# The order of TensorE and VectorE written out for the last depthwise tile and the layer norm behind it

## The chip, the cores and the metric

The kernel runs on one core of a Trainium2 chip, as one program. The metric is the device time of one execution, in microseconds (us), as the median of the runs shown. TensorE is called PE, VectorE DVE, ScalarE ACT, GpSimd POOL and the engine that issues the DMAs SP, as the profile calls them.

## The reference, cut to what matters

One step of a hybrid backbone of two layers with model width 1024, over 1024 sample tokens and 128 prompt tokens. Layer 0 mixes with a Conformer convolution, layer 1 with attention; both have a convolutional feed-forward behind the mixer. The change is in the Conformer mixer of layer 0:

```
def layernorm(x, g, b):
    mu = mean(x, -1)
    xc = x - mu
    y = xc * rsqrt(mean(xc * xc, -1) + EPS)
    return y * g + b

def conformer_conv(h, w_pw1, dw_w, dw_b, ln_g, ln_b, w_pw2):
    a, g = split(h @ w_pw1, 2, axis=-1)        # 1024 -> 2 x 1024
    u = a * sigmoid(g)
    u = dwconv(u, dw_w, dw_b)                  # 31 taps over the tokens, per feature
    u = silu(layernorm(u, ln_g, ln_b))         # mean and variance over the 1024 features
    return u @ w_pw2                           # 1024 -> 1024
```

Around it: `h = modulate(rmsnorm(x, norm1_g), sh1, sc1)`, then `x = x + g1 * y`. The vectors `sh1, sc1, g1, ...` of both layers come from `silu(cond) @ ada_w + ada_b` (adaLN).

## The kernel before, in words

**Layout.** Features lie on the partitions, tokens along the columns. The 1152 tokens are cut into three chunks of 384 (`c` = 0, 1, 2), the 1024 features into eight tiles of 128 (`j` = 0 to 7). Chunk 2 holds the last 256 sample tokens and the 128 prompt tokens. Products of weights take three matrix products each, high and low parts in a rounded float32 format (`mm3`, L247 to L249): one product of a tile with one chunk has 3 x 8 = 24 entries on PE. The products of the depthwise taps, of the means and of adaLN are in plain float32; each stands in the trace as two entries.

**The stage.** For each feature tile `gated(j, c)` computes the two pointwise products and the gated tile `u`. Then the 31 taps of the tile are summed: for tiles 0 to 6 the first 19 on DVE into `da` (L658, L660, all tokens at once, 1167 columns with the padding between samples and prompt), the other 12 on ACT and POOL into `pacc` (L645 to L651), and `join` (L666) adds the two into `U[c][:, j]`. `da` lies in a PSUM slot of which there is one (`acc`), so a tile's taps begin when the tile before is joined.

Tile 7, the last, is cut differently. 16 of its taps are products with diagonal matrices on PE (`diag`, L699; `dl`, L706), one PSUM bank per chunk; DVE adds seven taps on top of them (L660, `dl`), 384 columns a chunk (399 for chunk 2), ACT and POOL do eight (`pacc7`).

**The norm of a chunk.** The mean over the features is eight products with a matrix of 1/1024 (`mu`): those of tiles 0 to 6 in a loop ahead of the norm (L722, called the mean's head here, 14 entries), that of tile 7 in `layer_norm` (L726, the mean's tail, 2 entries). Then DVE subtracts the mean in two halves of four tiles (L731), ACT squares (L738), DVE and POOL add the squares (L741, L744), PE sums them over the partitions (`token_rstd`, L325, 12 entries), DVE scales (L332), POOL takes the power -1/2 (L334), PE spreads the result to all partitions (`spread`, L342, 6 entries), DVE multiplies (L753), ACT does Silu with gain and bias (L757) and a copy that is the high part `ln_h` (L760), and DVE subtracts it for the low part `ln_l` (L762). With both parts the last products of the mixer start (`pw2p`, eight feature tiles `m` for each chunk), with the residual on DVE (L384).

PSUM has in this stage four banks under `mm` (`dl` of three chunks, the mean of chunk 0, the sums of each norm, and then the `pw2p` products), one slot of three banks under `acc` (`da`, later the means of chunks 1 and 2) and one bank under `ms` (adaLN).

**What sets the order.** A planner at build time places the instructions on each engine by its own model of the times and by their order in the program; on the chip each engine then takes them in that fixed order and waits by semaphores. `tc.manual_schedule(engines=...)` keeps the program's order for the instructions that stand inside it on the engines named. In the kernel before it is used for SP in the whole program and for PE in the attention. The norms are generators in a list `bg`; `tick()` lets each take one step, and it is called after each of tile 7's taps on DVE and after each product:

```
    for c in range(NCH):
        for _ in taps_vector(last, u, dl[c], te, *SPAN[c], False):
            tick()
        join(last, dl[c], pacc, c, SPAN[c][0])
        bg.append(layer_norm(c))
        if c == 0:
            tick()
```

The adaLN products (`ada`, L270) of later layers run in the same stage, as their weights arrive (L258), and were traced ahead of it; so were the splits of weights into high and low parts (L220 on ACT, L221 on DVE) up to the first of `pw2p`; the later ones are traced behind it.

Of the kernel before, what the change touches and what calls it, by code (L numbers as in the profile page):

```python
# [11 lines left out]
ALU = mybir.AluOpType  # L12
# [55 lines left out]
def pieces(c):  # L68
    """A chunk's columns by the conditioning of their tokens."""
    lo, hi = c * CH, (c + 1) * CH  # L70
    out = []
    if lo < NS:
        out.append((0, min(hi, NS) - lo, 0))
    if hi > NS:
        out.append((max(lo, NS) - lo, CH, 1))
    return out
# [3 lines left out]
def tile_hybrid_step(ctx: ExitStack, tc: tile.TileContext, a: dict, outs: list):  # L80
# [17 lines left out]
    def phase(**slots):  # L98
        """SBUF of a phase: so many tiles of so many columns for each tag."""
        stack = ExitStack()  # L100
        pools = {
            tag: (stack.enter_context(tc.tile_pool(name=f"s_{tag}", bufs=bufs, reuse_waits="tile")), n)
            for tag, (bufs, n) in slots.items()
        }

        def tile_(tag, name, dt=F32, n=None):
            pool_, cols_ = pools[tag]
            return pool_.tile([P, n or cols_], dt, tag=tag, name=name)

        return stack, tile_  # L110
# [15 lines left out]
    class Banks:  # L126
        """PSUM, cut anew for some phases."""

# [16 lines left out]

    # work that runs beside the products, a step after each of them
    bg = []
# [22 lines left out]

    # ---- weights, in the order of their use: loads run up to three tiles ahead, the split into hi + lo (both exact
    # in float32r) one or two ----
    def ffn_order(l):
# [25 lines left out]
    class Weights:  # L199
# [24 lines left out]
        def ahead(self, splits, loads):  # L224
            """Has everything up to so many tiles from the next one split or loaded."""
            for i in range(self.at, min(self.at + max(splits, loads), len(self.order))):
                if self.order[i][0] == "stop":
                    break
                if i < self.at + loads and i not in self.raw and i not in self.ready:
                    self.load(i)  # L230
                if i < self.at + splits and i not in self.ready:
                    self.split(i)
# [17 lines left out]

# [1 line left out]
    def ada(pool, l, grp):  # L252
# [55 lines left out]

# [1 line left out]
    def add_stat(acc, j, c, src, eng=None, tag=None):  # L310
# [8 lines left out]
    def token_rstd(pool, parts, name, bank=None):  # L319
        """Sums over features of all parts[f, token], then (mean + eps) ** -0.5, tokens on partitions."""  # L320
        n = CH // P
        ps = pool("ms", f"{name}_s") if bank is None else bank[:, CH:]
        for t in range(n):
            for i, x in enumerate(parts):
                nc.tensor.matmul(  # L325
                    ps[:, t : t + 1], x[:, t * P : (t + 1) * P], ones, start=(i == 0), stop=(i == len(parts) - 1)
                )
        return rstd_of(ps[:, 0:n], 1.0 / D, n, name)
# [8 lines left out]
    def spread(pool, v, name, bank=None):  # L337
        """v[token, t] to every partition, tokens along the columns."""
        n = v.shape[1]
        ps = pool("ms", f"{name}_b") if bank is None else bank  # L340
        for t in range(n):
            nc.tensor.matmul(  # L342
                ps[:, t * P : (t + 1) * P], v[:, t : t + 1].to_broadcast([P, P]), ident, start=True, stop=True
            )
        return ps[:, 0 : n * P]
# [44 lines left out]

# [1 line left out]
    def ffn(pool, H, X, l, name, beside, done):  # L392
# [87 lines left out]

    # =========================== layer 0 ===========================
    pool.open(mm=(4, 512), acc=(1, 1536), ms=(1, 512))

# [1 line left out]
    vec_rows = [  # L485
# [36 lines left out]
    def load_x(c):  # L522
        """A chunk's tokens, on partitions, where the low parts of the normed chunks go later."""
        n = CH // P
        toks = hp.tile([P, n, D], F32, tag="hl", name=f"xt{c}")
        for t in range(n):
            tt = c * n + t
            nc.sync.dma_start(
                toks[:, t, :], a["x_sample"][0, tt * P : (tt + 1) * P, :] if tt < NS // P else a["x_prompt"][0]
            )  # L530
        return toks
# [45 lines left out]

    # conformer: gated pointwise, depthwise over tokens, layernorm, silu, pointwise
    us = []

    def gated(j, c):
        """The products of a chunk; yields before their gating."""
        if c == 0:
# [58 lines left out]
    def taps_pool(j, u, pacc, t0, s0_, s1_):  # L642
        """The taps from t0 on, with the bias."""
        d = pacc[:, s0_:s1_]
# [8 lines left out]
    def taps_vector(j, u, d, n, s0_, s1_, fresh):  # L653
        """The first n taps."""
        for t in range(n):
# [15 lines left out]
    for j in range(last + 1):  # L671
# [14 lines left out]
        taps_pool(j, u, pacc, t0, 0, CONV_N)  # L686
        for _ in taps_vector(j, u, da[:, 0:CONV_N], t0, 0, CONV_N, True):
            pass
        for c in range(NCH):
            join(j, da, pacc, c)  # L690

    # the last tile: some taps as products with diagonals, the others on top of them, chunk by chunk, so that the norm
    # of a chunk runs beside the taps of the next
    u = us[last][2]
# [5 lines left out]
    dl = []  # L700
    for c in range(NCH):
        s0_, s1_ = SPAN[c]
        dl.append(pool("mm", f"dl{c}")[:, 0 : s1_ - s0_])
        for i in range(PE_TAPS):
# [3 lines left out]
            )  # L708

    L = [None] * NCH  # L710
    half = KT // 2
    mus = []
    for c in range(NCH):
        if c == 0:
# [6 lines left out]
        for j in range(last):  # L721
            nc.tensor.matmul(mus[c], mean_w, U[c][:, j, :], start=(j == 0), stop=False)  # L722

    def layer_norm(c):
# [4 lines left out]
        for g in range(2):  # L729
# [3 lines left out]
            )  # L733
            eng = (nc.vector, nc.gpsimd)[g]
            for i in range(half // 2):
                sq = slot("tmp", f"lnsq{c}_{g}_{i}")[:, 0 : 2 * CH]
# [8 lines left out]
            yield  # L745
        yield
        bank = pool("mm", f"lnv{c}")
        rs = token_rstd(pool, ss, f"lnv{c}", bank)
        yield
        pb = spread(pool, rs, f"lnv{c}", bank)  # L750
        for g in range(2):
            jj = slice(g * half, (g + 1) * half)
            nc.vector.tensor_tensor(  # L753
                U[c][:, jj, :], U[c][:, jj, :], pb.unsqueeze(1).to_broadcast([P, half, CH]), ALU.mult
            )
            for j in range(g * half, (g + 1) * half):
                nc.scalar.activation(  # L757
                    U[c][:, j, :], U[c][:, j, :], AF.Silu, scale=col("conv_ln_g", j), bias=col("conv_ln_b", j)
                )
            nc.scalar.activation(hh[:, jj, :], U[c][:, jj, :], AF.Copy)  # L760
            yield
            nc.vector.tensor_tensor(hl[:, jj, :], U[c][:, jj, :], raw32(hh)[:, jj, :], ALU.subtract)  # L762
# [5 lines left out]
    for c in range(NCH):  # L768
# [4 lines left out]
        if c == 0:  # L773
            tick()

    def project_residual(H, X, c, acc, l, name, tag):
# [29 lines left out]

    # =========================== layer 1 ===========================
    # rotary tables with the norm gains folded in, tokens on partitions; gains: plain, halves swapped and signed
    NB = NS // P + 1
# [59 lines left out]
    def head_norm(ps, which, tt, name):  # L869
        """RMS norm of two heads, rotary unless they are the prompt's; yields between its stages."""  # L870
        ss = tiny(f"{name}ss", 2)
# [37 lines left out]
    def place(b, tt, o):  # L909
        """Heads to [feature, token]."""  # L910
        pt = pool("t", f"ptqk{b}_{tt}")
# [14 lines left out]

    # each slot: the products of a tile, then a further stage of each tile before it, the oldest first
    stages = []
# [50 lines left out]

    # the prompt's queries see the prompt's own keys: the four heads of a group at once  # L980
    def prompt():
# [54 lines left out]

    # samples: blocks of one head and the queries of one chunk, in steps of 128 queries; the scores run two steps
    # ahead of the transposes, the product with V one block behind them
    blocks = [(c, h) for c in range(NCH) for h in range(NH)]
# [27 lines left out]
    def softmax(s, st):  # L1067
        """Yields before each part of its exponential."""
        v = st["v"]
# [121 lines left out]

    # final norm, back to tokens on partitions
    gfs = []
# [44 lines left out]
def _rope_table():  # L1238
    """cos and sin by position on the 64-wide grid: [128, 2, 9, 32]; block t < 8 is the row part of token tile t,
    block 8 the column part, which all tiles share."""  # L1240
    import numpy as np
# [34 lines left out]
```

## Time and profile before

| | us |
|---|---|
| median of 3 runs | 2791.1 (2790.43 to 2793.83) |
| span of the profiled execution (its own time) | 2789.3 |
| PE busy | 2724.6 (98%) |
| DVE busy | 1585.4 (57%) |
| ACT busy | 1053.5 (38%) |
| POOL busy | 699.6 (25%) |
| the chain that ended last, share on PE | 94% |

The profiled execution has its time shown as a span, from the first to the last instruction; what lies around it is not in the profile. The span is 1.8 us below the median of the runs. Busy shares are means over the whole span, in which stages with different limits follow one another: the stage of the change lies between 333 and 425 us. "Granted clock" is TensorE's clock by the profile, as a share of full speed; its two levels are 1.2 and 2.4 GHz. In a timeline several instructions of one kind in a row are merged (x20 is twenty), and in brackets stands how long the engine had been idle before and what ended that. A few per cent of the matrix products are missing from a trace.

### The profile page before, as it was taken

Reading aid. Unit: us, or ns where it says so; the run is one execution under the profiler, and the core shown is the slowest. Engines: PE = TensorE matmul, PEld = TensorE weight load, DVE = VectorE, ACT = ScalarE, POOL = GpSimd, SP = SyncE. Lnnn points to the kernel's source line nnn. Section 1 sums busy time; section 2 is a strip of 40 time slices with the busy share of each in tenths; the row PEclk is TensorE's granted clock in tenths of the full one; section 3 lists DMA queues with packets and bytes.
Section 4 is the critical chain, followed back from the end, with each engine's and each line's share of the span. In section 5 each row is a group of like instructions: output and inputs, shape, how many; then the busy total and the mean of one; then the engine's idle time right before and its main releaser. Section 6 shows DMA issues by size and latency. Waiting matters only on the chain.

```text
span 2789.3 us, 40007 instructions
## 1 busy us (share of the span) xinstructions
PE 2724.6 (98%) x15959; PEld 2577.1 (92%) x15959; DVE 1585.4 (57%) x2743; ACT 1053.5 (38%) x2066; POOL 699.6 (25%) x782
## 2 busy tenths in 40 slices
PE   7999989999999999999999899999999999999999
PEld 4867649999999999999999799899999999999998
DVE  6878886544444444445643788766544444444445
ACT  5545546422222221222555777755422122221222
POOL 2777744300000000000555566535000000000003
PEclk9999989999999999999999999999999999999999
DMA  7465425311111111111210000044111111111111
GB/s 261 158 185 160 154 91 176 110 32 46 46 46 46 39 46 38 46 38 46 95 58 1 1 1 1 32 129 136 45 40 46 38 46 39 46 39 45 32 53 69
DMA packets 194419, 192.18 MB, mean 69 GB/s; under 512 B 7072, under 2 KB 173323, under 8 KB 192698
## 3 DMA queue, kind: packets, MB, share of 16 engines
q1 hardware_dynamic: 193946, 189.53, 21.7%
q8 instruction: 126, 2.06, 0.3%
q14 instruction: 59, 0.48, 0.1%
q0 software_dynamic: 288, 0.11, 0.0%
HBM read 175.19 MB, written 14.42 MB: 68 GB/s over the span
## 4 chain that ended last, share of the span: by engine, by line
PE 94%; DVE 3%; DMA 1%; ACT 1%; issue 0%; POOL 0%; SPq 0%; DVEq 0%; ACTq 0%; POOLq 0%
PE f1pd L249 3%; PE f1pd L247 3%; PE f1pd L248 3%; PE f1pg L249 3%; PE f0pg L249 3%; PE f1pg L248 3%; PE f0pg L248 3%; PE f0pv L247 3%; PE f0pg L247 3%; PE f1pv L249 3%; PE f1pg L247 3%; PE f0pv L248 3%; PE f1pv L248 3%; PE f1pv L247 3%; PE f0pv L249 3%; PE f0pd L248 3%
## 5 line engine op out<-in xcount | busy, mean ns | idle before, releaser
L220 ACT ACTIVATE w_hi<-w_raw 128x1024 fp32r<-128x1024 f32 x208 | 218.1, 1058 | 939.4 <-PE f0pd L248 223.7
L221 DVE TENSOR_TENSOR w_lo<-w_raw,w_hi 128x1024 fp32r<-128x1024 f32 x208 | 269.4, 1304 | 425.0 <-ACT w_hi L220 422.4
L651 POOL TENSOR_TENSOR pacc<-pacc,tmp 128x1167 f32<-128x1167 f32 (+2 forms) x98 | 234.2, 2393 | 64.8 <-ACT tmp L650 41.6
L384 DVE SCALAR_TENSOR_TENSOR x<-f1pd,mods,x 128x256 f32<-128x256 f32 (+1 forms) x352 | 170.2, 514 | 102.6 <-PE f1pd L249 102.4
L384 DVE SCALAR_TENSOR_TENSOR x<-f0pd,mods,x 128x256 f32<-128x256 f32 (+1 forms) x352 | 169.8, 514 | 99.1 <-PE f0pd L249 98.9
L660 DVE SCALAR_TENSOR_TENSOR da<-u,dww,da 128x1167 f32<-128x1167 f32 x126 | 180.8, 1435 | 2.8
L1084 POOL TENSOR_TENSOR pr<-pr,sm 128x384 f32<-128x384 f32 x192 | 153.8, 829 | 107.3 <-DVE sm L1082 49.4
L411 POOL MEMSET f1gp<- 128x1 f32 x66 | 3.7, 98 | 703.7 <-DVE f1gp L435 690.5
L411 POOL MEMSET f0gp<- 128x1 f32 x66 | 3.6, 98 | 703.8 <-DVE f0gp L435 690.7
L248 PE MATMUL f1pd<-f1al,w_hi 128*128 128x384 f32 x528 | 178.8, 339 | 0.0
L249 PE MATMUL f1pd<-f1ah,w_lo 128*128 128x384 f32 x528 | 178.7, 338 | 0.0
L249 PE MATMUL f0pd<-f0ah,w_lo 128*128 128x384 f32 x528 | 178.7, 338 | 0.0
L248 PE MATMUL f0pd<-f0al,w_hi 128*128 128x384 f32 x528 | 178.5, 338 | 0.0
L247 PE MATMUL f1pd<-f1ah,w_hi 128*128 128x384 f32 x528 | 178.5, 339 | 0.0
L247 PE MATMUL f0pd<-f0ah,w_hi 128*128 128x384 f32 x528 | 178.0, 338 | 0.0
L249 PE MATMUL f0pg<-n_h,w_lo 128*128 128x384 f32 x528 | 176.7, 335 | 0.0
L249 PE MATMUL f1pg<-n_h,w_lo 128*128 128x384 f32 x528 | 176.7, 335 | 0.0
L248 PE MATMUL f1pg<-n_l,w_hi 128*128 128x384 f32 x528 | 176.7, 335 | 0.0
L248 PE MATMUL f0pv<-n_l,w_hi 128*128 128x384 f32 x528 | 176.7, 335 | 0.0
L248 PE MATMUL f0pg<-n_l,w_hi 128*128 128x384 f32 x528 | 176.7, 335 | 0.0
L247 PE MATMUL f0pg<-n_h,w_hi 128*128 128x384 f32 x528 | 176.7, 335 | 0.0
L247 PE MATMUL f1pg<-n_h,w_hi 128*128 128x384 f32 x528 | 176.7, 335 | 0.0
(327 smaller groups left out, 7802.7 us busy)
## 6 DMA issues: line engine op xcount, KB each, us to landing
adaw<-in_ada_w_dram SPq DMA_DIRECT2D x96, 512.0 KB, 4.4
w_raw<-in_ffn_w_up_dram SPq DMA_DIRECT2D x88, 512.0 KB, 3.8
w_raw<-in_ffn_w_down_dram SPq DMA_DIRECT2D x44, 512.0 KB, 3.9
w_raw<-in_conv_w_pw_dram SPq DMA_DIRECT2D x40, 512.0 KB, 6.8
w_raw<-in_attn_w_o_dram SPq DMA_DIRECT2D x24, 512.0 KB, 4.4
xs_d<-x SPq DMA_DIRECT2D x6, 1536.0 KB, 11.1
x<-xs_d SPq DMA_DIRECT2D x6, 1536.0 KB, 7.8
w_raw<-in_attn_w_qkv_dram SPq DMA_DIRECT2D x12, 512.0 KB, 3.6
```

The costliest lines, as they stand in the source:

```text
L220: nc.scalar.activation(hi, raw, AF.Copy)
L221: nc.vector.tensor_tensor(lo, raw, raw32(hi), ALU.subtract)
L247: nc.tensor.matmul(ps, wh, mh, start=first, stop=False)
L248: nc.tensor.matmul(ps, wh, ml, start=False, stop=False)
L249: nc.tensor.matmul(ps, wl, mh, start=False, stop=last)
L384: nc.vector.scalar_tensor_tensor(xx, ps[:, lo:hi], mod(l, v, j, cond), xx, ALU.mult, ALU.add)
L411: nc.gpsimd.memset(gp[:, z : z + 1], 0.0)
L651: nc.gpsimd.tensor_tensor(d, d, tmp, ALU.add)
L660: nc.vector.scalar_tensor_tensor(d, src, tap(j, t), d, ALU.mult, ALU.add)
L1084: nc.gpsimd.tensor_tensor(pr[n], pr[n], ri.to_broadcast([P, CH]), ALU.mult)
```

## The change

The taps of tile 6 on DVE and their joins become a function `on_vector`, which is called inside a new block with the order of DVE and PE written out, `vector`. In that block the program's order is: tile 6's taps and joins; the diagonal products of tile 7 for chunks 0 and 1; the mean's head of chunk 0; tile 7's taps of chunk 0, their join, and the first step of chunk 0's norm (the mean's tail and the subtraction); the diagonal products of chunk 2; the mean's heads of chunks 1 and 2; and then tile 7's taps of chunks 1 and 2 with a step of a norm after each. Before, all diagonal products stood ahead of all mean's heads, and the planner chose the order.

In `layer_norm` the squares alternate between the two halves, with one step for each pair of squares; for chunk 0 the multiplication, the Silu, the copy and the low part go in quarters of two feature tiles instead of halves of four. For chunks 1 and 2 the halves stay. The rest of the diff takes comments and docstrings out.

```diff
--- before
+++ after
@@ -684,13 +684,18 @@
         pacc = slot("pacc", f"pacc{j}")
         t0 = TAPS - (POOL_TAPS if j < last - 1 else POOL_TAPS_6)
         taps_pool(j, u, pacc, t0, 0, CONV_N)
-        for _ in taps_vector(j, u, da[:, 0:CONV_N], t0, 0, CONV_N, True):
-            pass
-        for c in range(NCH):
-            join(j, da, pacc, c)
-
+        def on_vector(j=j, u=u, da=da, pacc=pacc, t0=t0):
+            for _ in taps_vector(j, u, da[:, 0:CONV_N], t0, 0, CONV_N, True):
+                pass
+            for c in range(NCH):
+                join(j, da, pacc, c)
+        if j < last - 1:
+            on_vector()
     u = us[last][2]
     t0 = TAPS - POOL_TAPS_7
     te = t0 - PE_TAPS
@@ -698,7 +703,8 @@
     for i in range(PE_TAPS):
         nc.scalar.activation(diag[:, i, :], ident, AF.Copy, scale=tap(last, te + i))
     dl = []
-    for c in range(NCH):
+    def taps_tensor(c):
         s0_, s1_ = SPAN[c]
         dl.append(pool("mm", f"dl{c}")[:, 0 : s1_ - s0_])
         for i in range(PE_TAPS):
@@ -707,10 +713,19 @@
                 dl[c], diag[:, i, :], u[:, s0_ + t : s1_ + t], start=(i == 0), stop=(i == PE_TAPS - 1)
             )
 
+    vector = ExitStack()
+    vector.enter_context(tc.manual_schedule(engines={mybir.EngineType.DVE, mybir.EngineType.PE}))
+    on_vector()
+    for c in range(NCH - 1):
+        taps_tensor(c)
     L = [None] * NCH
     half = KT // 2
     mus = []
-    for c in range(NCH):
+    def mean_head(c):
+        nonlocal mu_all
         if c == 0:
             mu = pool("mm", "mu0")
         else:
@@ -721,6 +736,9 @@
         for j in range(last):
             nc.tensor.matmul(mus[c], mean_w, U[c][:, j, :], start=(j == 0), stop=False)
 
+    mu_all = None
+    mean_head(0)
     def layer_norm(c):
         mu = mus[c]
         nc.tensor.matmul(mu, mean_w, U[c][:, KT - 1, :], start=False, stop=True)
@@ -731,8 +749,10 @@
             nc.vector.tensor_tensor(
                 U[c][:, jj, :], U[c][:, jj, :], mu.unsqueeze(1).to_broadcast([P, half, CH]), ALU.subtract
             )
-            eng = (nc.vector, nc.gpsimd)[g]
-            for i in range(half // 2):
+        yield
+        for i in range(half // 2):
+            for g in range(2):
+                eng = (nc.vector, nc.gpsimd)[g]
                 sq = slot("tmp", f"lnsq{c}_{g}_{i}")[:, 0 : 2 * CH]
                 j0 = g * half + 2 * i
                 nc.scalar.activation(sq.rearrange("p (j t) -> p j t", t=CH), U[c][:, j0 : j0 + 2, :], AF.Square)
@@ -743,22 +763,30 @@
                     for o in (0, CH):
                         eng.tensor_tensor(ss[g], ss[g], sq[:, o : o + CH], ALU.add)
             yield
-        yield
         bank = pool("mm", f"lnv{c}")
         rs = token_rstd(pool, ss, f"lnv{c}", bank)
         yield
         pb = spread(pool, rs, f"lnv{c}", bank)
-        for g in range(2):
-            jj = slice(g * half, (g + 1) * half)
+        n = 2 if c == 0 else half
+        for j0 in range(0, KT, n):
+            jj = slice(j0, j0 + n)
             nc.vector.tensor_tensor(
-                U[c][:, jj, :], U[c][:, jj, :], pb.unsqueeze(1).to_broadcast([P, half, CH]), ALU.mult
-            )
-            for j in range(g * half, (g + 1) * half):
+                U[c][:, jj, :], U[c][:, jj, :], pb.unsqueeze(1).to_broadcast([P, n, CH]), ALU.mult
+            )
+            for j in range(j0, j0 + n):
                 nc.scalar.activation(
                     U[c][:, j, :], U[c][:, j, :], AF.Silu, scale=col("conv_ln_g", j), bias=col("conv_ln_b", j)
                 )
             nc.scalar.activation(hh[:, jj, :], U[c][:, jj, :], AF.Copy)
-            yield
+            if c or j0 % half:
+                yield
+            if c == 0 and j0:
+                pp = slice(j0 - n, j0)
+                nc.vector.tensor_tensor(hl[:, pp, :], U[c][:, pp, :], raw32(hh)[:, pp, :], ALU.subtract)
+            if c:
+                nc.vector.tensor_tensor(hl[:, jj, :], U[c][:, jj, :], raw32(hh)[:, jj, :], ALU.subtract)
+        if c == 0:
             nc.vector.tensor_tensor(hl[:, jj, :], U[c][:, jj, :], raw32(hh)[:, jj, :], ALU.subtract)
         L[c] = (hh, hl)
 
@@ -772,6 +800,11 @@
         bg.append(layer_norm(c))
         if c == 0:
             tick()
+            taps_tensor(NCH - 1)
+            for i in range(1, NCH):
+                mean_head(i)
+    vector.close()
 
     def project_residual(H, X, c, acc, l, name, tag):
         for m in range(KT):
```

## Rows read from the trace of the kernel before

**Rows 1.** The page's first line.
```profile
span 2789.3 us, 40007 instructions
```
**Rows 2.** Table by stretches: window, busy us and instructions by engine, granted clock, DMA.
```profile
393.00:405.00 12.00, 6.98 (x35) 4.61 (x33) 8.63 (x13) 3.52 (x6) 5.62 (x6) 0.87 0.00 0
405.00:417.00 12.00, 5.86 (x21) 4.89 (x21) 10.06 (x10) 11.95 (x16) 2.05 (x2) 0.50 0.01 2
417.00:429.00 12.00, 11.98 (x55) 11.98 (x56) 6.84 (x6) 8.10 (x11) 0.00 (x0) 0.77 0.84 254
```
**Rows 3.** Timeline of PE: start, us, line, operation, out<-in, count, idle before.
```profile
333.42 3.39 PE L706 MATMUL dl<-u,diag 128*128 128x384 f32 x10
...
340.20 6.72 PE L706 MATMUL dl<-u,diag 128*128 128x384 f32 x20
...
369.64 1.05 PE L270 MATMUL ada<-adaw,cs 128*32 128x512 f32 x4
...
385.32 5.32 PE L722 MATMUL mu<-u,mean_w 128*128 128x384 f32 x16
390.57 1.05 PE L270 MATMUL ada<-adaw,cs 128*32 128x512 f32 x4
...
396.61 1.40 PE L325 MATMUL lnv<-ones,lnss 128*128 128x1 f32 x12
...
405.87 2.29 PE L325 MATMUL lnv<-ones,lnss 128*128 128x1 f32 x10 [0.28 <-POOL lnss L744]
410.19 1.65 PE L342 MATMUL lnv<-ident,lnv_r 128*128 128x128 f32 x6 [2.02 <-POOL lnv_r L334]
414.32 1.33 PE L247 MATMUL pw2p<-ln_h,w_hi 128*128 128x384 f32 x3 [2.48 <-ACT ln_h L760]
417.02 0.69 PE L248 MATMUL pw2p<-ln_l,w_hi 128*128 128x384 f32 x1 [1.37 <-DVE ln_l L762]
...
423.42 0.33 PE L249 MATMUL pw2p<-ln_h,w_lo 128*128 128x384 f32 x1
```
**Rows 4.** Chain that ended last, in order of time: chunk 2's sums and spread.
```profile
437.33 1.01 PE lnv L325 x10
...
442.96 0.67 PE lnv L342 x6
```
**Rows 5.** Timeline of DVE, 336 to 417 us.
```profile
336.26 1.44 DVE L658 TENSOR_SCALAR da<-u,dww 128x1167 f32<-128x1167 f32 x1
337.73 8.81 DVE L660 SCALAR_TENSOR_TENSOR da<-u,dww,da 128x1167 f32<-128x1167 f32 x6
346.44 0.61 DVE L660 SCALAR_TENSOR_TENSOR dl<-u,dww,dl 128x384 f32<-128x384 f32 x1
...
366.35 1.23 DVE L221 TENSOR_TENSOR w_lo<-w_raw,w_hi 128x1024 fp32r<-128x1024 f32 x1
...
378.53 1.54 DVE L666 TENSOR_TENSOR u<-da,pacc 128x384 f32<-128x384 f32 x4
...
404.87 3.42 DVE L753 TENSOR_TENSOR u<-u,lnv 128x1536 f32<-128x1536 f32 x2
...
415.21 3.42 DVE L762 TENSOR_TENSOR ln_l<-u,ln_h 128x1536 fp32r<-128x1536 f32 x2
```
**Rows 6.** Timeline of PE at the end of the attention.
```profile
1834.85 0.42 PE L247 MATMUL wop<-ao_h,w_hi 128*128 128x384 f32 x1
...
1839.18 0.28 PE L247 MATMUL po<-pT_h,vh 128*128 128x256 f32 x1
```
**Rows 7.** Timeline of POOL: the power of chunk 1.
```profile
408.90 1.24 POOL L334 TENSOR_TENSOR lnv_r<-lnv_m,mhalf 128x3 f32<-128x3 f32 x1 [3.08 <-DVE lnv_m L332]
```
**Rows 8.** Timeline of ACT: the Silu and copies of chunk 0.
```profile
406.71 1.28 ACT L757 ACT_TABLE_LOAD   x1
408.00 4.89 ACT L757 ACTIVATE u<-u,vecs 128x384 f32<-128x384 f32 x8
412.80 2.84 ACT L760 ACTIVATE ln_h<-u 128x1536 fp32r<-128x1536 f32 x2
```

## The prediction

> **What bounds the kernel now.** I read the page first: PE is busy almost to the end of a 2789.3 us span [rows 1], so only a stage in which PE stands still can give anything. The table by stretches shows one such stage, the end of the first mixer. Between 393 and 417 us PE is busy 6.98 + 5.86 of 24 us, and the granted clock falls from 0.87 to 0.50, its lower level, and is back at 0.77 over the next stretch [rows 2]. After that PE does not stop before the feed-forward, so whatever is saved here moves the end one for one, unless a new stop appears behind it.
>
> Then PE in order of time [rows 3]. Its last pointwise product ends at 333.42. From there it runs without a gap through the depthwise products of the last tile (`dl`), the adaLN products (`ada`) and the mean products (`mu`) until 396.61, when the sums of chunk 0's norm (`lnv`) begin. From there it waits, by the releasers in brackets, for VectorE, GpSimd and ScalarE in turn; the first `pw2p` product starts at 414.32, goes on at 417.02, and the 24 entries of one product are through at about 423.3.
>
> Of these 26.7 us (396.61 to 423.3) the work itself is, at full clock: sums and spread of chunks 0 and 1, 2 x (1.01 + 0.67) [rows 4]; one mean tail of two entries, 0.65 [rows 3]; 24 product entries at 0.175, 4.2. That is 8.2, so 18.5 us are lost. That is the most that the change can give.
>
> **The change, part by part.**
>
> *Tile 6 first on VectorE.* Now VectorE alternates tile 6's taps (`da`) with tile 7's (`dl`), and tile 6 is joined only at 378.53 [rows 5]. Its taps start at 336.26, behind the join of tile 5, which the change does not touch. With the order written out they run alone: 19 taps at (8.81 - 1.43) / 5 = 1.476, 28.0, to 364.3; four joins, 1.54, to 365.8; seven taps of chunk 0 at about 0.6, 4.2; one join, 0.55: 370.6. Two weight splits (the one shown and another) came ready at 366 to 369. They stand outside the written order. I read what becomes of such instructions from the attention, whose TensorE order is written out too: `wop` products that follow that block in the code run at 1834.85, ahead of `po` products of the block at 1839.18 [rows 6]. So others still slip in between, and I add the two splits, 2.4 together: chunk 0's last mean product can start at about 373.2. Bounds: 370.8 without the splits, 374 with waits beside them.
>
> *PE until then.* Two chunks of `dl`, 64 entries at about 0.333, 21.3; chunk 0's mean head, 14 at 0.325, 4.6; `ada`, whose groups take about 0.98 each and of which nine of 14, the one at 369.64 the ninth, had run by 370, 8.9 [rows 3]; gaps 0.7. From 333.42 this gives 369: PE waits some 4 us that it does not wait today. Bounds: 0, if `ada` fills it, to 5.
>
> *PE behind it, in the written order.* Mean tail 0.65, third chunk of `dl` 32 x 0.345 (399 columns instead of 384) = 11.0, two mean heads 28 x 0.325 = 9.1, five groups of `ada` and its transposes 5.3: 26.1, about 400 for the start of chunk 0's sums. This is the cover that the change puts over the subtraction, squares and sums of chunk 0: from 373.9 these need 3.4 for the subtraction, which has the shape of the multiplication [rows 5], and, as an estimate, four squares and the additions between them some 7, done by about 385.
>
> *Sums to spread.* The sums end at 401.2. For chunk 1 today the sums end at 408.16, the power starts at 408.90 and takes 1.24, and the spread of 1.65 ends at 411.84 [rows 3, 7]: 3.7. With PE at full clock at its start I take 3.5: 404.7. Bounds 2.8 to 3.7.
>
> *Norm in quarters.* Today halves: multiplication 1.7, the eight Silu, both copies, then the low part 1.7 [rows 5, 8]. The change has quarters of 768 columns: multiplication 0.87, two Silu 1.25, copy 0.78, so the first high part is there 3.0 after the spread, the first low part 3.9 after. The later quarters follow at ScalarE's pace, two Silu and a copy, 1.95; the last low part is at 9.75. PE is fed six entries per quarter; at the low clock it needs 1.92 for them, so it is just kept busy. I let the low clock last until the fourth quarter; the last six then take about 1.2: 24 entries done 11.1 after the spread, 415.8. Bounds: 10.7 if the clock never falls, and 2.5 us more than I take if 17 further entries run at 0.32 instead of 0.175, as they do from 417.02 today.
>
> The table load of 1.28 ahead of the first Silu [rows 8] goes into ScalarE's idle time between squares and Silu, and costs nothing. The Trainium skill ("ScalarE: Activation LUTs", What ACT_TABLE_LOAD costs) counts a drain of about 1.38 us beside the load. The trace does not agree here: the first Silu starts at 408.00, where the load of 406.71 ends. By the page's 2.66 us, an estimate, and with the load uncovered, the first product would come that much later and the gain would be 1.8 us, which is the last rival's case below.
>
> *What is put off.* The mean tails of chunks 1 and 2 (4 entries, 1.3) and chunk 1's sums and spread (1.7) were behind PE at 423.3 and are now still to be done: 3.0. VectorE still owes four taps of chunk 1, seven of chunk 2 and both norms; I cost that at nothing as long as chunk 1's norm is ready before its products start, and price the other case below. The other order of the squares moves the same instructions at equal cost. No DMA is added or moved past a queue; the reload of chunk 0's tokens follows its norm's last low part as before.
>
> *Sum.* 423.3 - 415.8 - 3.0 = 4.5 us. The profiled span of 2789.3 becomes 2784.8. The median of the runs shown, 2791.1, stands 1.8 above the span; the same 4.5 gives 2786.6.
>
> **Rivals.**
>
> *More of the 18.5 comes back.* If the splits do not slip in (2.4), `ada` fills the wait ahead of the mean (up to 4), PE keeps its clock, or PE takes entries of the next products between quarters (as the three leading entries at 414.32 seem to do), the gain is 6 to 10: 2781 to 2785. For it: the planner still places `ada` and the products freely. Against: `ada` comes in steps of its loads, and the banks that a second product needs are held by `dl` and chunk 0's spread.
>
> *VectorE's head of line: slower.* In the written order the scaling of chunk 0's sums stands ahead of all that VectorE still owes, and it waits for PE's sums behind the third `dl` and two mean heads. So VectorE, busy 8.63 and 10.06 of 12 us in these stretches today [rows 2], stands idle from about 383 to 401. The Trainium skill ("PSUM — Partial Sum Buffer", Engine vs sequencer instructions) has VectorE's queue as strictly first in, first out; by that rule nothing written behind the scaling can overtake it, and this rival lives on it. Chunk 1's norm then starts at 414, behind chunk 0's. With subtraction 3.4, squares and sums 6, spread 3.5, and in halves 1.7 + 2.5 + 1.45 + 1.7 each, one after the other, plus six taps and some 8 us of splits and residuals in between, it ends at about 447 to 449. Its products are due at 415.8 + 7 x 4.2 + 3.0 = 448, their second half 2 later: it decides from some 450 on. If it is 10 us late (ScalarE's splits and squares between its Silu), PE waits 10 there: 2791.1 - 4.5 + 10 = 2797. Against: PE can take the first half of three products first, 6 us of cover.
>
> *The change doesn't reach PE.* Chunk 0's sums are still behind nearly all of PE's `dl` and `mu` work (about 400 against 396.61 today), and if the wait ahead of the mean is 8 us, not 4, only the quarters' gain is left: 2789 to 2792.
>
> **How the numbers follow.** Forecast (gain 2 to 6): 0.42. More comes back: 0.35. VectorE late: 0.17. No effect: 0.06. The bound of 0.2% (about what a measurement of this kernel can tell from no change) is 5.6 us, 2785.5. Of the forecast 0.06 lies beyond it, with the 0.35 that is 0.41 faster; of the slow rival 0.14 lies above 2796.7; the rest, 0.45, is within. The range, 2781 to 2793, holds both gains, the case without effect and the small end of the slow one; the forecast's own range is 2785 to 2789.
>
> **What would show it.** Right: tile 6's join at about 364; chunk 0's last mean product near 373, behind a PE wait of about 4 us; sums near 400; first `pw2p` entry at 407 to 408; one product through near 416; no wait of PE at chunk 1's first product. Wrong: sums before 396 or after 403; a PE wait for chunk 1's `ln_h` or `ln_l` near 448; `pw2p` waiting for a bank or a split; `ada` placed so that PE waits for its loads.

## The result, and the profile after

The changed kernel takes 2823.1 us (median of 3 runs, 2820.44 to 2826.13), the kernel before 2791.1: a ratio of 1.012, 95% interval 1.0105 to 1.0134. It is 32 us slower by the medians, and outside the range of 2781 to 2793. The span of the profiled execution:

```profile
span 2818.6 us, 40015 instructions
```

The first feed-forward product starts at 554.4 us instead of 523.7, 30.7 later; at the end of the span 29.3 are left. So the whole loss lies ahead of the feed-forward, in the stage of the change: from its first `dl` product (332.22, and 333.42 before) to the first feed-forward product it takes 222.2 us instead of 190.3, 31.9 more. The table by stretches of the changed kernel (window, length, busy us and instructions of PE, its weight loads, DVE, ACT, POOL; granted clock, DMA share, GB/s), the first three to be held against [rows 2]:

```profile
393.00:405.00 12.00, 10.81 (x45) 6.99 (x43) 0.69 (x2) 0.00 (x0) 0.86 (x1) 1.00 0.00 0
405.00:417.00 12.00, 0.00 (x0) 0.00 (x0) 8.88 (x11) 8.15 (x12) 0.00 (x0) 0.58 0.00 0
417.00:429.00 12.00, 4.69 (x12) 3.57 (x13) 7.75 (x10) 3.37 (x4) 2.99 (x3) 0.50 0.87 264
453.00:465.00 12.00, 2.07 (x4) 0.93 (x5) 7.29 (x8) 4.17 (x6) 2.58 (x3) 0.50 0.10 29
```

Ahead of 405 the change does what it says: PE is busy 10.81 of 12 us instead of 6.98. Then PE does nothing at all for a whole stretch (0.00 of 12), little in the next, and stands a second time from 447.2 (the start at 455.35 below, less its 8.19 of idle time). The timeline of PE says for whom (start, us, line, operation, count; in brackets the idle time before and its releaser), against [rows 3]:

```profile
332.22 3.39 PE L712 MATMUL dl<-u,diag 128*128 128x384 f32 x10
...
378.10 0.66 PE L283 MATMUL adat<-ident,adar 128*128 128x128 f32 x4 [0.70 <-ACT adar L279]
380.97 0.91 PE L744 MATMUL mu<-u,mean_w 128*128 128x384 f32 x2 [2.22 <-DVE u L666]
381.72 10.89 PE L712 MATMUL dl<-u,diag 128*128 128x399 f32 x32
392.45 9.19 PE L737 MATMUL mu<-u,mean_w 128*128 128x384 f32 x28
401.48 1.40 PE L325 MATMUL lnv<-ones,lnss 128*128 128x1 f32 x12
404.07 0.93 PE L342 MATMUL lnv<-ident,lnv_r 128*128 128x128 f32 x6 [1.19 <-POOL lnv_r L334]
417.64 1.65 PE L744 MATMUL mu<-u,mean_w 128*128 128x384 f32 x2 [12.64 <-DVE u L666]
425.96 0.56 PE L325 MATMUL lnv<-ones,lnss 128*128 128x1 f32 x2 [6.67 <-DVE lnss L764]
426.38 0.67 PE L247 MATMUL pw2p<-ln_h,w_hi 128*128 128x384 f32 x1
...
432.34 1.17 PE L325 MATMUL lnv<-ones,lnss 128*128 128x1 f32 x10
...
455.35 1.65 PE L744 MATMUL mu<-u,mean_w 128*128 128x384 f32 x2 [8.19 <-DVE u L666]
464.58 0.59 PE L325 MATMUL lnv<-ones,lnss 128*128 128x1 f32 x2 [7.58 <-DVE lnss L764]
465.02 0.67 PE L247 MATMUL pw2p<-ln_h,w_hi 128*128 128x384 f32 x1
```

Chunk 0 is spread by 405.0, where it was expected. But what comes next on PE is not its first `pw2p` product; it is chunk 1's mean tail, 12.64 later, and chunk 1's first sum, 6.67 after that. Only then does `pw2p` start, at 426.38, 12 us later than before (414.32). The same happens to the fifth product, behind the tail and the first sum of chunk 2 (8.19 and 7.58). The input of `pw2p` had long been there, as the timeline of DVE shows, against [rows 5]:

```profile
365.79 1.23 DVE L221 TENSOR_TENSOR w_lo<-w_raw,w_hi 128x1024 fp32r<-128x1024 f32 x1 [5.72 <-ACT w_hi L220]
...
371.72 1.55 DVE L666 TENSOR_TENSOR u<-da,pacc 128x384 f32<-128x384 f32 x4
...
378.79 0.26 DVE L287 TENSOR_TENSOR mods<-adat,adab 128x16 f32<-128x16 f32 x2 [2.36 <-PE adat L283]
...
380.36 0.56 DVE L666 TENSOR_TENSOR u<-dl,pacc 128x384 f32<-128x384 f32 x1
...
402.91 0.16 DVE L332 TENSOR_SCALAR lnv_m<-lnv 128x3 f32<-128x3 f32 x1 [13.98 <-PE lnv L325]
402.99 0.61 DVE L660 SCALAR_TENSOR_TENSOR dl<-u,dww,dl 128x384 f32<-128x384 f32 x1
...
409.29 0.96 DVE L786 TENSOR_TENSOR ln_l<-u,ln_h 128x768 fp32r<-128x768 f32 x1 [1.90 <-ACT ln_h L781]
...
415.43 0.96 DVE L790 TENSOR_TENSOR ln_l<-u,ln_h 128x768 fp32r<-128x768 f32 x1 [1.11 <-ACT ln_h L781]
...
417.03 0.56 DVE L666 TENSOR_TENSOR u<-dl,pacc 128x384 f32<-128x384 f32 x1
419.33 3.42 DVE L749 TENSOR_TENSOR u<-u,mu 128x1536 f32<-128x1536 f32 x2 [1.20 <-PE mu L744]
```

The first low part of chunk 0 ends at 410.2, the last at 416.4. DVE had waited 13.98 us at chunk 0's scaling (L332), with the last four of tile 7's seven taps of chunk 1 written behind it (three had run between 385 and 389), so that chunk 1 is joined at 417.0 and subtracted from 419.3.

The ledger of PE, as what it loses between 367 and 470: 6.2 ahead of chunk 0's last mean product, 1.2 ahead of the spread, 12.6 + 6.7 and 8.2 + 7.6 at the later chunks' tails and sums, and behind these stops the low clock: 2.0 for 13 product entries at 0.32 apart instead of 0.175, 1.5 for those from 465 on, and two tails of 1.65 instead of 0.81, 1.7. The sum is 47.7 against the 18.5 of before: 29.2 more. Of the stage's 31.9 us this leaves 2.7 without a line in the ledger; that 29.2 comes so near to the difference of the spans (29.3) is chance.

### The profile page after: what moved, and what is told of

It is laid out like the page before. It is cut to its first block, busy times and chain, and to the rows that moved or that the text cites. A ratio compares the mean times of both kernels' runs of the same rounds, so it can differ in the third digit from the quotient of the medians.

```text
span 2818.6 us, 40015 instructions
## 1 busy us (share of the span) xinstructions
PE 2722.3 (97%) x15959; PEld 2572.0 (91%) x15959; DVE 1584.7 (56%) x2747; ACT 1053.8 (37%) x2068; POOL 698.9 (25%) x782
## 4 chain that ended last, share of the span: by engine, by line
PE 92%; DVE 4%; ACT 1%; DMA 1%; issue 1%; POOL 0%; SPq 0%; DVEq 0%; POOLq 0%; ACTq 0%
PE f1pd L249 3%; PE f1pd L247 3%; PE f1pd L248 3%; PE f0pg L249 3%; PE f1pg L249 3%; PE f1pg L248 3%; PE f0pg L248 3%; PE f0pv L248 3%; PE f1pg L247 3%; PE f1pv L248 3%; PE f1pv L247 3%; PE f0pg L247 3%; PE f0pv L247 3%; PE f1pv L249 3%; PE f0pv L249 3%; PE f0pd L247 3%
## 5 line engine op out<-in xcount | busy, mean ns | idle before, releaser
L248 PE MATMUL f1pv<-n_l,w_hi 128*128 128x384 f32 x528 | 176.5, 334 | 0.0
```

The costliest lines, as they stand in the source:

```text
L248: nc.tensor.matmul(ps, wh, ml, start=False, stop=False)
```

## The experiments

Each ratio below is to the kernel before as timed beside that run; its medians were 2788.5 to 2790.6 there. Where two runs are compared in us by their medians, 2 us can come from that alone.

Why does a product whose operands are ready stand behind sums of another chunk? My theory: its place on PE was fixed at build time, by a PSUM bank. In program order the sums of chunks 1 and 2 (`lnv1`, `lnv2`) take a bank of `mm` ahead of the products `pw2p0_0` and `pw2p0_4`, as the order of PE's instructions shows:

```
before:  lnv0 sums, mean tail 2, lnv0 spread, lnv1 sums, lnv1 spread, pw2p0_0 ... 0_3, lnv2 sum (1), pw2p0_4
after:   lnv0 sums, lnv0 spread, mean tail 1, lnv1 sum (1), pw2p0_0 ... 0_3 (the other lnv1 sums among them), mean tail 2, lnv2 sum (1), pw2p0_4
```

In neither does `pw2p0_0` stand ahead of the first `lnv1` sum, nor `pw2p0_4` ahead of `lnv2`. Before, that was harmless: chunk 1's sums were through at 408.16, ahead of `pw2p`'s input. The rival: the banks don't matter, and the loss is VectorE's written order alone (its head of line), whatever the bank.

**The bank, in the changed kernel.** The later sums go into the bank that their chunk's mean holds already:

```diff
-        bank = pool("mm", f"lnv{c}")
+        bank = mu_all[:, c] if c else pool("mm", f"lnv{c}")
```

> The changed kernel, but the norms of chunks 1 and 2 take the bank of their own mean for sums and spread, instead of a bank of the ring that the pw2p products use too. Bank theory (the ring's banks are handed out in program order, so the first pw2p product cannot be placed ahead of chunk 1's sums, nor the fifth ahead of chunk 2's): pw2p starts 4 to 6 us after chunk 0's spread, at 409 to 411 instead of 426.4; the PE waits of 12.6, 6.7, 8.2 and 7.6 us go, some 30 of 35 us come back: 2788 to 2798. Rival (the written order itself puts PE's instructions of the later norms ahead of the products, whatever the banks): pw2p still behind chunk 1's sums, 2818 to 2826. Rival (the inputs of pw2p are late, VectorE's work): pw2p starts at 416 or later, about 2810.

2807.5 us, ratio 1.0053 (1.0038 to 1.0069): 15.6 of the 32 us are back (18.7 by the ratios), not the 30 expected. In PE's order `pw2p0_0` and `pw2p0_1` now stand directly behind chunk 0's spread, and PE waits for this chunk's own norm instead (timeline of PE):

```profile
409.10 0.93 PE L342 MATMUL lnv<-ident,lnv_r 128*128 128x128 f32 x6 [1.19 <-POOL lnv_r L334]
414.34 0.69 PE L247 MATMUL pw2p<-ln_h,w_hi 128*128 128x384 f32 x1 [4.31 <-ACT ln_h L781]
```

That shows the bank as about half of the loss. The four waits of the change are gone, but the first product comes at 414.34, not at 409 to 411: chunk 0's spread itself is 5 us later than in the changed kernel (404.07), 1.3 of it because the stage begins later (333.48 against 332.22). Of the 17 us that are left over the kernel before, the largest wait that is new is one for weight splits (waits of PE, 300 to 700 us, total, times, longest):

```profile
PE pw2p L247 <- ACT w_hi L220: 7.2, 5, 3.5
```

**The bank, in the kernel before.** The same line there.

> The kernel before with the bank change alone (chunks 1 and 2 take sums and spread in their mean's bank). Bank theory: in the kernel before chunk 1's norm was early enough, its sums run at 405 to 408 while the first pw2p product has its input only at 414, so the bank order costs nothing there: 2787 to 2793, same. If the bank of the mean were better for another reason (one bank more for the products), this kernel would be faster by 5 us or more, below 2785, and the gain of e1_bank would not be the order's.

2786.5 us, ratio 0.9991 (0.998 to 1.0001): no difference that can be told. In these runs the bank costs only where a later chunk's norm is late.

**A shorter written order.** The block ends behind the mean heads instead of behind all of tile 7's taps, the bank as in the change:

```diff
                 mean_head(i)
-    vector.close()
+            vector.close()
```

> The changed kernel, but the block with the written order ends behind the mean's heads, so that the later chunks' taps and norms are ordered by the planner again; the banks as in the changed kernel. Bank theory: chunk 1's subtraction and squares move into VectorE's idle 14 us (389 to 403), chunk 1's sums come at about 405 to 408, and the products right behind them, at 409 to 412: 2790 to 2800. Rival (VectorE's work is late in itself): sums of chunk 1 not before 420, 2815 or more.

2810.8 us, ratio 1.0071 (1.0056 to 1.0086), between the two expectations. Chunk 1's tail comes early (the first line below; the second is chunk 2's tail), but its sums come at 421.49, no sooner than the rival had them, and still hold the products back (timeline of PE; 11.11 the second time):

```profile
407.15 0.89 PE L744 MATMUL mu<-u,mean_w 128*128 128x384 f32 x2
...
411.56 1.65 PE L744 MATMUL mu<-u,mean_w 128*128 128x384 f32 x2 [2.14 <-DVE u L749]
421.49 0.59 PE L325 MATMUL lnv<-ones,lnss 128*128 128x1 f32 x2 [8.29 <-DVE lnss L764]
```

**The norm's new body alone.** The kernel before with the quarters and the new order of squares, nothing written out.

> The kernel before with only the new body of the norm: squares alternating, chunk 0 in quarters; no written order. My prediction's term for the quarters: chunk 0's first product starts some 2 to 3 us sooner, the end 0 to 4 us: 2787 to 2792. Rival (the quarters cost: more and smaller instructions on ScalarE and VectorE): 2792 to 2797.

2797.4 us, ratio 1.0025 (1.0014 to 1.0036), where my term for the quarters gave 2787 to 2792. This part alone already makes the kernel slower, at the same place, with no written order of VectorE (waits of PE):

```profile
PE lnv L325 <- DVE lnss L746: 15.9, 2, 9.2
```

**The same with the bank edit.**

> The kernel before with the new body of the norm (as e3_body) and the bank change. In e3_body PE waited 6.7 us at chunk 1's sums and 9.2 us at chunk 2's, with pw2p products behind them. Bank theory: the second wait goes, the first goes or halves: 2783 to 2791. If the new body is slower by its own instructions: 2794 to 2799 as e3_body.

2785.9 us, ratio 0.9989 (0.998 to 0.9999): both waits are gone, and 11.5 us with them (10.0 by the ratios). So the quarters do not cost by their own instructions, and that rival falls. Twice, then, the one line takes the waits away, once with a written order and once without, and where the later norm is early it changes nothing; so the rival that leaves the banks out falls. Which part of the new body makes the later sums late, the quarters or the order of the squares, was not tried.

**Only TensorE's order written** (the engines' set without DVE), the bank as in the change.

> The changed kernel with the order written out for TensorE alone; VectorE is ordered by the planner. If VectorE's written order makes chunk 1's norm late (bank theory with VectorE's head of line as its cause): chunk 1's sums follow chunk 0's spread within 5 us and pw2p starts at 410 to 414, 2792 to 2802. If TensorE's written order alone is the cost: 2815 to 2826.

2809.1 us, ratio 1.0064 (1.0044 to 1.0085): 14 us below the change, so VectorE's written order does cost, but the time lies between the two expectations: the sums, and chunk 2's tail ahead of them (the second line), still hold `pw2p` (waits of PE):

```profile
PE lnv L325 <- DVE lnss L764: 16.6, 2, 8.7
PE mu L744 <- DVE u L749: 6.3, 1, 6.3
```

**Tile 6 in place**, ahead of the block.

> The changed kernel, but tile 6's taps and joins stand ahead of the block, so that the planner mixes them as before. If writing them out is what costs (chunk 0's last mean product came at 381.0, not at 373 as I forecast): that product moves by more than 3 us to either side. Bank theory: the order behind it is the same (chunk 1's sums ahead of pw2p), so the end stays within 6 us of the changed kernel: 2817 to 2829.

2820.1 us, ratio 1.0108 (1.0092 to 1.0124); the last mean product of chunk 0 at 382.21, the four later waits as in the change (12.65, 6.67, 8.20, 7.58). That product comes 47.1 us behind the stage's first `dl` product (335.15), against 48.8 in the change. Here, where the products wait for other sums, writing out tile 6 is neither the cost nor a gain.

**Two weight splits off VectorE.** The low parts of the two tiles that fall between tile 6's taps are made on GpSimd:

```diff
-            nc.vector.tensor_tensor(lo, raw, raw32(hi), ALU.subtract)
+            eng = nc.gpsimd if i in (17, 18) else nc.vector
+            eng.tensor_tensor(lo, raw, raw32(hi), ALU.subtract)
```

> The changed kernel with the low parts of two weight tiles (the two that VectorE split between tile 6's taps and its joins, or near them) made on GpSimd instead of VectorE. If VectorE's wait of 5.72 us for such a split is what moved the last mean product of chunk 0 from the predicted 373 to 381: it starts at 375 (373.5 to 377) and chunk 0's sums start at 397 to 399 instead of 401.5. By the bank theory this is worth little at the end, since the first product waits for chunk 1's sums, which wait for VectorE: 2817 to 2821 against 2823. If instead the time follows the first chunk's mean: 4 to 6 us less, 2817 or below, with the first pw2p product as much earlier.

2822.5 us, ratio 1.0119 (1.0104 to 1.0135). The expected 375 for chunk 0's last mean product was a miss: VectorE did get through early, but the mean product did not follow (its timeline, then PE's):

```profile
363.61 1.55 DVE L667 TENSOR_TENSOR u<-da,pacc 128x384 f32<-128x384 f32 x4
...
369.74 0.56 DVE L667 TENSOR_TENSOR u<-dl,pacc 128x384 f32<-128x384 f32 x1
```

```profile
373.22 4.02 PE L271 MATMUL ada<-adaw,cs 128*32 128x512 f32 x12 [2.32 <-DMA adaw<-in_ada_w_dram]
378.70 1.05 PE L271 MATMUL ada<-adaw,cs 128*32 128x512 f32 x4 [1.46 <-DMA adaw<-in_ada_w_dram]
380.45 0.66 PE L284 MATMUL adat<-ident,adar 128*128 128x128 f32 x4 [0.70 <-ACT adar L280]
380.94 0.81 PE L745 MATMUL mu<-u,mean_w 128*128 128x384 f32 x2
```

Chunk 0 is joined at 370.3, and its mean product starts at 380.94, as before this edit (380.97). PE has adaLN's products and transposes ahead of it, and these wait for their loads. In the changed kernel they reached that product through VectorE too: `mods` (L287), which reads the transposes, stood among chunk 0's taps, and VectorE waited 2.36 us for it at 378.79.

**Bank and reload.** On top of the bank edit, the reload of a chunk's tokens (L388) is issued behind the take of its first product's weights, not ahead of it.

> e1_bank, and the reload of a chunk's tokens is issued on SP behind the loads of the first product's take instead of ahead of them, so that the weights of the fourth product do not queue behind it. In e1_bank PE waited 8.2 us for the split of weights whose loads stood on SP behind that reload, which waits for the last low part of the chunk's norm. SP queue theory: these waits at 429 to 434 shrink to 0 to 3 and those at chunk 1 likewise: 2798 to 2804 (e1_bank 2807.5). Rival (the splits are late on ScalarE and VectorE): same as e1_bank.

2803.1 us, ratio 1.0051 (1.0035 to 1.0067). The wait for splits goes from 7.2 to 1.8 us and the span from 2805.9 to 2800.7; by the ratios the two kernels cannot be told apart. PE waits 5.1 us more for the high and low parts of the norms instead (9.9 against 4.8).

**Bank and shorter order; and both with the reload.**

> The changed kernel with two edits at once: the sums of chunks 1 and 2 lie in the bank of their own mean, and the written order ends behind the first chunk's mean heads (the chunk's loop, with its taps on VectorE and the norms of chunks 1 and 2, is left to the planner). If the bank holds back the products and the written order of VectorE is only a second, smaller cost: neither of the two waits of the bank edit alone nor those of the shorter order alone may stand, the first pw2p product comes at 412 to 416 without a wait for sums of squares, and the time is 2788 to 2800, below both single edits (2807.5 and 2810.8). If the two edits take away the same thing, the time stays at 2804 to 2811. If the written order is worth something by itself once the banks are out of the way: below 2786.

> As the run before, and the reload of a chunk's tokens issued behind the take of its first product's weights, so that the weight loads don't queue behind it on SP. If what is left after bank and shorter order is the late weight split: 3 to 5 us below the run before (the reload alone gave 4.5 on top of the bank edit), that is 2785 to 2796. If the late split was itself a result of the longer written order: within 1.5 us of the run before.

2798.9 us, ratio 1.0033 (1.0021 to 1.0045), and 2797.9, ratio 1.0027 (1.0018 to 1.0036). Each edit gives something beside the other, but less than their sum: 24.2 us by the medians, where they give 15.6 and 12.3 alone. The reload brings nothing measurable more (1.0 us by the medians), as the second expectation had it: with the shorter order no wait for a split's high part was left that it could take away. Both kernels start `pw2p` late, since ScalarE takes chunk 1's squares, and a table load behind them, ahead of chunk 0's Silu, and VectorE chunk 1's subtraction (410.95, 3.42 us, with bank and shorter order) ahead of chunk 0's multiplication (414.28). ScalarE with bank and shorter order, and PE's wait for it:

```profile
412.80 0.84 ACT L758 ACTIVATE lnsq<-u 128x768 f32<-128x768 f32 x1 [19.08 <-DVE u L749]
414.48 0.84 ACT L758 ACTIVATE lnsq<-u 128x768 f32<-128x768 f32 x1 [0.84 <-DVE u L749]
415.34 1.28 ACT L778 ACT_TABLE_LOAD   x1
```

```profile
420.66 1.33 PE L247 MATMUL pw2p<-ln_h,w_hi 128*128 128x384 f32 x3 [8.38 <-ACT ln_h L781]
```

**No written order: body, bank and reload.**

> The kernel before with the new body of the norm (quarters for the first chunk, squares in the other order), the bank edit, and the reload behind the take of the first product's weights; no order written out. With the reload away from the weight loads the remaining waits for ScalarE's weight splits (2.4 us in the run without it) go: 2782 to 2785, 0.998 of before. If these waits are set by ScalarE itself and not by the loads, it is the same as without the reload, 2785 to 2788.

2781.2 us, ratio 0.997 (0.9959 to 0.9982), the fastest kernel of the study and, with the interval clear of 1, faster than the kernel before. The wait for splits is gone, as the first expectation had it; against the run without the reload the intervals overlap. Its PE, against [rows 3]: sums, spread, first product, 8.6 us ahead of the kernel before, of which 1.9 lie ahead of the stage (its first `dl` product starts at 331.51, not 333.42).

```profile
394.71 1.40 PE L325 MATMUL lnv<-ones,lnss 128*128 128x1 f32 x12
399.36 1.65 PE L342 MATMUL lnv<-ident,lnv_r 128*128 128x128 f32 x6 [3.26 <-POOL lnv_r L334]
...
405.75 1.33 PE L247 MATMUL pw2p<-ln_h,w_hi 128*128 128x384 f32 x3
```

**Whose written order costs the rest.** With bank, reload and the short block, the written order still costs 16.7 us (2797.9 against 2781.2). Three runs: the order written for TensorE alone, for VectorE alone, and for both but ended ahead of the mean heads of chunks 1 and 2.

> The changed kernel with the bank edit, the later reload and the short written order (as the run before of both), but the order is written for TensorE alone. The same without any written order takes 2781.2, with both engines written 2797.9: 16 us are the written order's own price. If it is TensorE's (20 us of other products put between the first chunk's mean and its sums of squares): 2793 to 2799, with the sums still at 400 or later. If it is VectorE's (its additions and taps held in program order): 2780 to 2786, with the sums before 397.

> The same, with the order written for VectorE alone. If the price is TensorE's order: 2780 to 2786. If it is VectorE's: 2793 to 2799. If the two engines' orders each cost a part, both runs lie at 2785 to 2793.

> Both engines written, bank edit and later reload, but the written order ends behind the last chunk's diagonal products, ahead of the mean heads of chunks 1 and 2 (9.2 us of PE's work), which the planner may then put behind the first chunk's sums. If the sums are late because of the work that is written between mean and sums: the sums come up to 9 us earlier than 405.8, and the time is 2785 to 2792. If the planner puts the heads ahead of the sums all the same, or the late weights and splits of the stretch before set the mean: 2795 to 2799.

2791.4 us (1.0003, 0.9994 to 1.0013), 2787.4 (0.9989, 0.9979 to 0.9999) and 2787.8 (0.9991, 0.9982 to 1.0001). Both runs of one engine lie at 2785 to 2793, so each engine's order costs a part: 10.2 us TensorE's, 6.2 VectorE's, by the medians. Taking the mean heads out of the block gives 10 us back. This splits the price by engine; by mechanism it is shown only in part. The first product in the three, in this order (timelines of PE):

```profile
412.45 1.33 PE L247 MATMUL pw2p<-ln_h,w_hi 128*128 128x384 f32 x3 [8.37 <-ACT ln_h L781]
```

```profile
408.54 1.33 PE L247 MATMUL pw2p<-ln_h,w_hi 128*128 128x384 f32 x3 [2.39 <-ACT ln_h L781]
```

```profile
410.21 1.33 PE L247 MATMUL pw2p<-ln_h,w_hi 128*128 128x384 f32 x3 [1.75 <-ACT ln_h L781]
```

The 8.4 us at chunk 0's high part stand in all three kernels in which TensorE's order covers the heads of chunks 1 and 2 and ends there, and in neither of the other two. In those three chunk 1's mean tail runs between chunk 0's sums and its spread (at 410.02, 407.08 and 401.81), so that chunk 1's subtraction and first squares fall ahead of chunk 0's multiplication and Silu; in the other two the tail runs ahead of the sums. That fits all five runs, but no run moves the tail alone, so it stays an observation. In the run whose block ends ahead of the heads chunk 0's sums came at 400.4, 5.4 earlier than with the block that ends behind them (405.8), not the 9 of the heads' whole length; but with TensorE alone written, heads and all, they came at 400.6 too, so the heads' place does not by itself make the sums late.

## Why the prediction was wrong, point by point

**The step that failed: "What is put off".** I cost VectorE's lateness with chunk 1 "at nothing as long as chunk 1's norm is ready before its products start". Chunk 1's norm was needed much sooner: ahead of chunk 0's first product, because of the bank. With it fell "first `pw2p` entry at 407 to 408", measured 426.4. I had read [rows 6] as showing that products from behind a written block slip in between, and did not ask what they need in order to be placed: the `wop` products ran, so they had their banks; `pw2p` had to stand behind `lnv1`. `pw2p` "waiting for a bank" stood in the list of what would be wrong, without a price. The bank edit takes 15.6 us off the changed kernel, 11.5 off the new body alone and, within the error, nothing off the kernel before.

That is about half of the 32 us. With the bank edit the written order of both engines still costs 21.6 us against the same norm without it (2807.5 and 2785.9), where the sum had a gain from it. With the later reload and the short block 16.7 us of it are left; the runs divide these by engine and show single waits in them (splits, adaLN's loads, chunk 1's norm ahead of chunk 0's); a full account of this half is open.

**The slow rival had the mechanism, not the place.** It said that VectorE would stand idle at the scaling until 401; it stood 13.98 us, to 402.9, and the taps of chunk 1 behind it came late. It was priced at chunk 1's products, from 450 on, with 6 us of cover and 10 of lateness. The price was due at chunk 0's first and fifth products, at 405 and 447, with no cover, and twice: 19.3 and 15.8 us. The fourth tap of chunk 1, the first that is written behind the scaling, ran at 402.99, right behind the scaling of 402.91. By that, the trace agrees with the rule cited there (the Trainium skill, "PSUM — Partial Sum Buffer", Engine vs sequencer instructions).

**Tile 6 on VectorE: the work right, the waits wrong.** Joined by 373.3 instead of 365.8, since VectorE stood 5.72 us before a weight split placed among the taps; the splits were counted by their work alone, 2.4. With the splits elsewhere tile 6 was joined at 365.2 and chunk 0 at 370.3, as worked out (365.8, 370.6).

**The last mean product: 381.0, not 373.2.** The splits are not the cause. I put five groups of adaLN behind this product; all ran ahead of it, the last seven from 366 to 378, with waits for their loads. The kernel before had this product at 384.7, so the change moved it by 3.7, not 11.5, and 1.2 of these 3.7 only because the stage began earlier.

**Sums and spread: right by two misses that cancel.** The groups that moved from behind to ahead cancel in the sum, and still the sums started at 401.5 (400). From their end at 402.9 to the end of the spread it took 2.1, below the bounds of 2.8 to 3.7 (3.5 taken). So the spread was done at 405.0 (404.7) by luck.

**Quarters: their steps 1.2 to 1.6 longer than taken.** The first high part came 4.2 after the spread (3.0), the last low part 11.4 (9.75): ScalarE did four Silu ahead of the first copy and VectorE the second quarter's multiplication ahead of the first low part. The table load cost nothing, as said; it ran at 388.25, in ScalarE's idle time.

**PE's clock.** It was at its lower level from the stop on (0.50 in the stretch from 417), as in [rows 2], but twice instead of once: 5.2 us in all where I had counted the first low stretch alone.

## What to carry to other kernels

Ask of each product that is to come earlier not only when its operands are ready but what was given a bank ahead of it in program order; here a slower requester of that ring, even of another chunk, held it back, and a bank that the requester already owned freed it. Moving work of one chunk ahead of another's on a written order moves the other's waits along: follow every instruction that is queued behind the new wait to its first reader on the busy engine. Try the smaller piece alone: here the new body of the norm with the bank edit and the later reload gave 0.997, and the written order on top of it 1.0027.

## What the hardware showed that was not expected

GpSimd makes the low part of a 128x1024 weight tile in 2.35 to 2.37 us, VectorE in 1.23; moving two of them there cost nothing that could be measured (2822.5 against 2823.1), in a kernel whose TensorE waits elsewhere. The load of ScalarE's table takes 1.28 us and runs ahead as soon as the squares are through (388.25 in the changed kernel, with Silu 16.5 us later), so in these runs it shows up on the path where squares of another chunk come just ahead of the Silu, as at 415.34 above.
